# Down projections of a two-layer decoder trunk: seven products for eight, with weight sums formed by adding DMAs

## The chip, the cores and the metric

The kernel runs on one NeuronCore of a Trainium2 chip. A core has a matrix engine (TensorE, "PE" in the profile, with its weight loads listed apart as "PEld"), a vector engine (VectorE, "DVE"), a scalar engine (ScalarE, "ACT"), GpSimd ("POOL") and a sync engine ("SP") that here only issues DMAs. Each engine works through its own instructions in order and waits on semaphores for the others. Data lie in HBM, in SBUF (128 partitions) and in PSUM (128 partitions by eight banks of 512 fp32 values), where matmul results appear.

The metric is device time in microseconds, the median of several runs. The profile shows one execution.

## The reference, cut to what matters

256 tokens of width 2048 go through two layers. Layer 0 mixes by gated linear attention, layer 1 by forgetting attention; both also attend to 256 memory tokens. Behind each mixer stands the channel mixer that matters here:

```python
def conv_ffn(h, w_up, conv_w, conv_b, w_down):
    u = causal_dwconv(h @ w_up, conv_w, conv_b)
    a, val = split_cols(u, [FFN_HIDDEN, FFN_HIDDEN])     # 5632 each
    return (jax.nn.silu(a) * val) @ w_down               # (256, 5632) @ (5632, 2048)
...
for i in range(DEPTH):                                   # 2 layers
    ...
    x = x + gla_mixer(...) or fox_mixer(...)
    h = rmsnorm(x, norm_ffn[i])
    x = x + conv_ffn(h, ffn_w_up[i], ffn_conv_w[i], ffn_conv_b[i], ffn_w_down[i])
return rmsnorm(x, norm_final)
```

All inputs and the output are fp32. The weights are far larger than the activations: each is read once from HBM and used for 256 tokens.

## The kernel before

**Precision.** A matmul takes a rounded fp32 type (fp32r). To keep fp32 accuracy every operand is split into a rounded part "hi" and the rest "lo", and a product is made of three: hi·hi, hi·lo and lo·hi. Weights come from one array `wp` in HBM, laid out in the order of use, in units of 128 x 1024 values (512 KB). `load_unit` (line 185) issues the load of a unit into `raw` on SP (line 196) and the cast to `whi` on ScalarE (line 199); `split_unit` (line 202) adds `wlo = raw - whi` on VectorE (line 208). `raw` has four buffers, `whi` and `wlo` three each.

**Projections.** `proj_fm` (line 211) gives its result with features on the partitions: weights are the stationary operand, the two halves of the activations (256 tokens hi, 256 tokens lo) the moving one; lines 233, 234 and 236 are its matmuls. `proj_tm` (line 246) gives tokens on the partitions: 128 tokens of a chunk are stationary, 512 columns of a weight unit move; for each chunk of 128 inputs and each of two token halves it issues three matmuls (lines 270 to 272) into one PSUM bank per token half.

**Channel mixer.** `ffn` (line 780) takes the 44 chunks of hidden features in three parts of 16, 16 and 12 (`PARTS`). In a part it first runs one up projection per chunk (`proj_fm`, gate and value side by side), then convolution, SiLU and product (lines 795 to 805), and `split` (lines 296 and 297) writes hi and lo of the chunk into the buffer `m`. After the last chunk of the part `add_out` (line 771) runs the down projection in four column blocks of 512: `proj_tm`, and then one addition of a PSUM bank into the residual `x[f]` per token half (line 774). In the last part of a layer a callback `then` also prepares what follows: `preparing` (line 812) sums squares, transposes `x` and splits it for the next stage, and at the end of the kernel the final norm and the stores (line 860).

**Buffers.** `bufA` and `bufB` are 16 tiles each of 128 x 2 x 256, and change roles between stages: one holds the input of a projection, the other takes the next activations. `mk` and `mv` hold memory keys and values of both layers for the whole kernel. `fox` (line 674) keeps its values in `vt`, which first serves as a stash for the transposed residual.

**Order.** The program is traced into a scheduler that orders each engine's instructions by priority and by a simulated timeline, gives out buffers in that order, and inserts the semaphore waits. `tc.high_priority(offset=AHEAD)` (line 203) moves loads and splits of weights 300 places ahead, so that they run as early as buffers allow. All weight loads go through SP's queue. GpSimd only clears a few tiles.

Of the kernel before, what the change touches and what calls it, by code (L numbers as in the profile page):

```python
# [12 lines left out]
F32 = mybir.dt.float32  # L13
# [27 lines left out]
OG_EARLY = 2  # L41
WARM = 8

FV_PARTS = ((0, 376), (376, 764), (764, 1152), (1152, 1536))


# [8 lines left out]
def _panels():  # L55

    full = list(range(KC))
    out = []  # L60

    def fm(key, w, c0, kcs=full, second=None):
        cols = [(c0, 256)] if second is None else [(c0, 128), (second, 128)]
        out.append((key, w, kcs, cols, 4))

    def tm(key, w, c0, n, kcs=full, more=()):
        out.append((key, w, kcs, [(c0, n), *more], 2))

    for l in range(2):
# [36 lines left out]
    for f in range(4):  # L106
        tm(("wo", 1, f), ("fox_w_out", 0), f * 512, 512, late)
    ffn(1)
    return out

# [21 lines left out]
C_N = C_BF + 1  # L132

M_ID, M_ONE, M_FOX, M_SCAN, M_LVL = 0, 128, 256, 512, 768
M_N = M_LVL + NVER * len(LEVELS)


@with_exitstack
def _trunk(ctx: ExitStack, tc: tile.TileContext, xt, xtok, memt, wp, wgu, gns, gfin, cnv, par, msk, out):
# [9 lines left out]

    gains = const.tile([P, G_N], F32, name="gains")  # L150
    part = const.tile([P, C_N], F32, name="part")
    mask = const.tile([P, M_N], F32, name="mask")
    ident = mask[:, M_ID : M_ID + P]
    ones = mask[:, M_ONE : M_ONE + P]
    foxmask = mask[:, M_FOX : M_FOX + T]
    scanmask = mask[:, M_SCAN : M_SCAN + T]

    def gain(name, i):
        c = C_GAIN[name] + i
# [3 lines left out]
    nc.gpsimd.memset(eps, EPS)  # L163

    x = [const.tile([P, 2, 512], F32, name=f"x{f}") for f in range(4)]
    bufA = [const.tile([P, 2, T], F32R, name=f"A{i}") for i in range(KC)]
    bufB = [const.tile([P, 2, T], F32R, name=f"B{i}") for i in range(KC)]
    mk = [const.tile([P, MEM_H, T], F32, name=f"mk{l}") for l in range(2)]
    mv = [const.tile([P, 2, MEM_H * HD], F32, name=f"mv{l}") for l in range(2)]


    with tc.high_priority(offset=2 * AHEAD):
        V.memset(bufB[KC - 1].bitcast(F32), 0.0)
        warm = pwork.tile([P, 512], F32, name="ps_o", tag="o", bufs=1)
        for i in range(WARM):
            TE.matmul(warm, bufB[KC - 1][:, 0, :P], bufB[KC - 1], start=i == 0, stop=i == WARM - 1)
# [69 lines left out]
    def proj_tm(key, src, evac, spare=None):  # L246
# [9 lines left out]
        for i in range(len(units) + ahead):  # L256
            for b, u in ((0, i), (1, i - ahead)):
# [14 lines left out]
                    TE.matmul(a, xk[:, 1, xs], hi[:, s], start=False, stop=last)  # L272
                if u == len(units) - 1:
                    evac(b, a)

    def turned(pool, bank, width, col):

# [132 lines left out]

    nrm = Norm(D, "m")
    nx = StreamNorm()
    with tc.tile_pool(name="load", bufs=1) as lp:
        mraw = [lp.tile([P, KC + 4 * T], F32, name=f"mt{i}") for i in range(4)]
        mt = [t[:, KC:].rearrange("p (c t) -> p c t", t=T) for t in mraw]
# [53 lines left out]
        with tc.issue_after(loads[-1].ins):  # L469
            for i in range(KC):  # L470
                nc.sync.dma_start(xf[i], xt[i])
            nc.sync.dma_start(part, par)
            nc.sync.dma_start(mask[:, M_FOX:], msk[:, M_FOX:])
        proj_tm(("mv", 0), bufA, mv_out(0))
        for i in range(KC):
            split(bufB, i, xf[i], gain("mix0", i))
        for j in range(2):
            proj_fm(("mk", 1, j), bufA, mk_out(1, j))
            if j == 0:
# [3 lines left out]
                for f in range(4):  # L483
                    for b in range(2):
                        nx.add(f, b)
        proj_tm(("mv", 1), bufA, mv_out(1))


    def gla(nx):
        h, mix = bufB, bufA  # L490
        with tc.tile_pool(name="gla", bufs=1) as gp:
# [53 lines left out]
            def core(hd, q, k, v, bc):  # L545
# [43 lines left out]
                for li, B in enumerate(LEVELS):  # L589
# [28 lines left out]
                    m3 = mask[:, M_LVL + NVER * li : M_LVL + NVER * (li + 1)].bitcast(I32)  # L618
# [52 lines left out]
                take_og(j)  # L671


    def fox(nx, vt):
        hk, hq, mix = bufB, bufA, bufB
        stash = vt.rearrange("p b (i t) -> p (b i) t", t=T)
        with (
            tc.tile_pool(name="fox", bufs=1) as fp,
            tc.tile_pool(name="foxd", bufs=1, space=bass.MemoryType.DRAM) as dp,
        ):  # L680
            cdram = dp.tile([FOX_H, T], F32, name="cdram")
            kt = fp.tile([P, FOX_H, T], F32, name="fkt")
            for j in range(6):
                proj_fm(("fk", j), hk, lambda c, a, j=j: V.tensor_tensor(kt[:, 2 * j + c, :], whole(a), nx.row(), ALU.mult))
                for i in range(2 * j, 2 * j + 2):
                    split(hq, i, stash[:, i, :], gain("mix1", i))
# [43 lines left out]
            def attend(hd, q):  # L730
# [7 lines left out]
                TE.matmul(ps[:, :P], q[:, :P], kt[:, hd, :P], start=True, stop=True)  # L738
                TE.matmul(ps[:, P : 3 * P], q[:, P:], kt[:, hd, :], start=True, stop=True)  # L739
                pt = work("t")  # L740
                for b in range(2):
                    n = (b + 1) * P
# [25 lines left out]
                take_q(j)  # L768


    def add_out(key, src, then=None, spare=None):
        for f in range(4):
            def evac(b, a, f=f):
# [3 lines left out]

            proj_tm((*key, f), src, evac, spare if f == 3 else None)

    def ffn(l, nx, h, m, then, spare=None):  # L780
        with tc.tile_pool(name=f"ffn{l}", bufs=1) as fp:
            cw = fp.tile([P, 4 * 88], F32, name="cw")
            nc.sync.dma_start(cw, cnv[l])
            us = [fp.tile([P, T + 2], F32, name=f"u{i}") for i in range(4)]
# [3 lines left out]
            for p, (lo, hi) in enumerate(PARTS):  # L788
                for j in range(lo, hi):
                    cv = {}  # L790

                    def evac(c, a, j=j, cv=cv, i=j - lo):
# [9 lines left out]
                        cv[c] = r  # L802
                        if c == 1:
                            S.activation(cv[0], cv[0], AF.Silu)
# [4 lines left out]
                end = p == len(PARTS) - 1  # L809
                add_out(("down", l, p), m, then if end else None, spare if end else None)  # L810

    def preparing(name, dst, also=None):
        n = StreamNorm()

        def then(f, b):
            n.add(f, b)
            if b == 0:
                return
            for i in range(4 * f, 4 * f + 4, 2):
                ps = work("s", 2)  # L820
# [10 lines left out]
        return n, then  # L831

    gla(nx)
    n, then = preparing("ffn0", bufB)
    add_out(("wo", 0), bufA, then)
    with tc.tile_pool(name="stash", bufs=1) as st:
        vt = st.tile([P, 2, FOX_H * HD], F32, name="fvt")

        def also(i, ps):
            if i < 12:  # L840
                S.activation(vt.rearrange("p b t -> p (b t)")[:, i * T : (i + 2) * T], ps, AF.Copy)
            else:
                for j in range(2):
                    split(bufA, i + j, ps[:, j * T : (j + 1) * T], gain("mix1", i + j))

        n2, then = preparing("kv", bufB, also)
        ffn(0, n, bufB, bufA, then)
        fox(n2, vt)
    n, then = preparing("ffn1", bufA)
    add_out(("wo", 1), bufB, then)  # L850


    fin = StreamNorm()
    with tc.tile_pool(name="store", bufs=1) as op:
        gf = op.tile([P, D], F32, name="gf")
        nc.sync.dma_start(gf, gfin.to_broadcast([P, D]))
        y = op.tile([P, 2, 512], F32, name="y")
        junk = op.tile([P, 1], F32, name="junk")

        def then(f, b):  # L860
            fin.add(f, b)
            if f == 0 and b == 0:
                S.activation(junk, fin.sums[:, 0, 0:1], AF.Sqrt)
            dst = y if f == 3 else x[f]
            V.tensor_tensor(dst[:, b, :], x[f][:, b, :], gf[:, f * 512 : (f + 1) * 512], ALU.mult)
            if f < 3:
# [7 lines left out]
            V.reciprocal(r, r)  # L874
            fin.newton(r, v, 1)
            for g in range(4):
                t = y[:, b, :] if g == 3 else x[g][:, b, :]
# [6 lines left out]
        ffn(1, n, bufA, bufB, then, op)  # L884


def _constants():
# [66 lines left out]
```

## Time and profile before

| | |
|---|---|
| median of 3 runs | 2302.16 us (2302.14 to 2302.43) |
| span of the profiled execution (first to last instruction) | 2300.7 us; the median lies 1.5 us above it |
| granted TensorE clock | 0.999 of full speed |
| bytes read from HBM | 425.87 MB |
| weight loads of 512 KB issued by SP | 743 |
| instructions | 33144 |

The first number of a group's row is its busy time, the second the mean duration of one, and behind the bar stands the idle time of the engine just before these instructions, with what ended it ("<-"). A row of the stage table gives, for a window, the busy time of each engine and the count of instructions in parentheses, the granted clock, the mean busy share of the 16 DMA engines, and GB/s. Matmuls overlap in the engine, so that the sum of their durations is more than the time they take. Down projections run at about 658 to 745, 924 to 1012, 1146 to 1211, 1740 to 1828, 2005 to 2093 and 2226 to 2292 us.

### The profile page before, as it was taken

What the parts mean: (1) busy time and instruction counts of PE and PEld (TensorE: products, weight loads), DVE (VectorE), ACT (ScalarE), POOL (GpSimd) and SP (SyncE); (2) the same over time, 40 slices, a digit from 0 to 9 for tenths busy, and PEclk for the clock granted to TensorE, in tenths of its full rate; (3) what the DMA queues carried; (4) which work ended last, traced back from release to release, by engine and by line L of the source; (5) the groups of instructions that cost most, each with busy time, mean ns of one, the idle gap of its engine ahead of it and who ended that gap; (6) DMA issues with size and microseconds to landing.
All of it is one profiled execution on the core that took longest, in us unless ns stands there. A gap on an engine that the chain in (4) does not pass through costs nothing.

```text
span 2300.7 us, 33144 instructions
## 1 busy us (share of the span) xinstructions
PE 2286.8 (99%) x12392; PEld 1977.8 (86%) x12392; DVE 1614.6 (70%) x2639; ACT 1252.9 (54%) x1961; POOL 3.0 (0%) x19
## 2 busy tenths in 40 slices
PE   9999999999999999999999999999999999999998
PEld 7889888888888888888888998888888888888886
DVE  7568987577765777557767557657776577756775
ACT  7555565555553555445565555556554455534554
POOL 0000000000000000000000000000000000000000
PEclk9999999999999999999999999999999999999999
DMA  8644455555555555555555564555555555555554
GB/s 317 196 160 160 150 165 177 187 182 190 190 190 194 187 191 189 192 191 189 190 183 185 180 194 158 166 191 188 186 191 192 192 187 189 190 195 191 186 190 156
DMA packets 124745, 430.15 MB, mean 187 GB/s; under 512 B 14108, under 2 KB 18600, under 8 KB 124456
## 3 DMA queue, kind: packets, MB, share of 16 engines
q1 hardware_dynamic: 124152, 427.24, 55.7%
q8 instruction: 97, 1.59, 0.3%
q10 hardware_dynamic: 432, 0.79, 0.1%
q14 instruction: 64, 0.52, 0.1%
HBM read 425.87 MB, written 2.11 MB: 186 GB/s over the span
## 4 chain that ended last, share of the span: by engine, by line
PE 99%; DMA 0%; ACT 0%; DVE 0%; issue 0%; SPq 0%; DVEq 0%; ACTq 0%
PE acc L233 37%; PE acc L234 20%; PE acc L271 12%; PE acc L272 12%; PE acc L270 12%; PE acc L236 2%; PE ps_s L825 0%; PE ps_s L614 0%; PE ps_t L388 0%; PE ps_s L395 0%; PE ps_o L406 0%; DMA mt<-memt 0%; PE ps_s L739 0%; PE ps_o L633 0%; PE ps_o L755 0%; PE ps_s L533 0%
## 5 line engine op out<-in xcount | busy, mean ns | idle before, releaser
L208 DVE TENSOR_TENSOR wlo<-raw,whi 128x1024 fp32r<-128x1024 f32 (+4 forms) x812 | 972.7, 1199 | 547.3 <-ACT whi L199 533.3
L199 ACT ACTIVATE whi<-raw 128x1024 fp32r<-128x1024 f32 (+4 forms) x812 | 843.5, 1040 | 775.7 <-PE acc L272 370.6
L233 PE MATMUL acc<-B,whi 128*128 128x512 f32 x1980 | 684.1, 396 | 0.0
L233 PE MATMUL acc<-A,whi 128*128 128x512 f32 x1680 | 579.1, 396 | 1.9 <-DVE A L300 1.5
L234 PE MATMUL acc<-B,wlo 128*128 128x256 f32 x2112 | 551.2, 281 | 0.0
L234 PE MATMUL acc<-A,wlo 128*128 128x256 f32 x1792 | 463.9, 281 | 0.7 <-DVE wlo L208 0.7
L233 PEld LDWEIGHTS acc<-B,whi 128*128 128x128 f32 x1980 | 360.9, 188 | 69.0
L234 PEld LDWEIGHTS acc<-B,wlo 128*128 128x128 f32 x2112 | 397.7, 188 | 21.7
L234 PEld LDWEIGHTS acc<-A,wlo 128*128 128x128 f32 x1792 | 337.3, 188 | 21.6 <-DVE wlo L208 1.7
L233 PEld LDWEIGHTS acc<-A,whi 128*128 128x128 f32 x1680 | 304.9, 188 | 58.8 <-DVE A L300 1.9
L271 PE MATMUL acc<-wlo,B 128*128 128x512 f32 (+3 forms) x736 | 274.9, 374 | 1.2 <-DVE wlo L208 1.2
L272 PE MATMUL acc<-whi,B 128*128 128x512 f32 (+3 forms) x736 | 274.0, 373 | 0.0
L270 PE MATMUL acc<-whi,B 128*128 128x512 f32 (+3 forms) x736 | 247.6, 372 | 0.0
L271 PE MATMUL acc<-wlo,A 128*128 128x512 f32 x544 | 212.6, 391 | 0.0
L272 PE MATMUL acc<-whi,A 128*128 128x512 f32 x544 | 211.8, 389 | 0.0
L270 PE MATMUL acc<-whi,A 128*128 128x512 f32 x544 | 192.6, 391 | 0.0
L241 ACT ACTIVATE part<-acc 128x256 f32<-128x256 f32 x240 | 90.0, 375 | 163.1 <-PE acc L236 163.1
L271 PEld LDWEIGHTS acc<-wlo,B 128*128 128x128 f32 x736 | 138.2, 188 | 21.0 <-DVE wlo L208 1.6
L272 PEld LDWEIGHTS acc<-whi,B 128*128 128x128 f32 x736 | 138.3, 188 | 18.7
L270 PEld LDWEIGHTS acc<-whi,B 128*128 128x128 f32 x736 | 137.5, 188 | 18.7
L243 DVE TENSOR_TENSOR wholes<-acc,part 128x256 f32<-128x256 f32 x240 | 101.1, 421 | 66.3 <-ACT part L241 65.9
L272 PEld LDWEIGHTS acc<-whi,A 128*128 128x128 f32 x544 | 102.2, 188 | 21.2
(201 smaller groups left out, 1571.2 us busy)
## 6 DMA issues: line engine op xcount, KB each, us to landing
raw<-wp SPq DMA_DIRECT2D x743, 512.0 KB, 3.5
raw<-wp SPq DMA_DIRECT2D x32, 384.0 KB, 3.1
raw<-wp SPq DMA_DIRECT2D x24, 388.0 KB, 3.5
raw<-wp SPq DMA_DIRECT2D x8, 400.0 KB, 3.0
xf<-xt SPq DMA_DIRECT2D x16, 128.0 KB, 4.5
x<-xtok SPq DMA_DIRECT2D x4, 512.0 KB, 6.7
mt<-memt SPq DMA_DIRECT2D x3, 512.0 KB, 7.1
cb<-cdram SPq DMA_DIRECT2D x12, 128.0 KB, 3.3
```

Source lines behind the costliest of these rows:

```text
L199: casts.append(S.activation(hi[:, s], raw[:, s], AF.Copy))
L208: V.tensor_tensor(lo[:, s], raw[:, s], hi[:, s].bitcast(F32), ALU.subtract)
L233: TE.matmul(a, hi[:, s], both, start=done == 0, stop=False)
L234: TE.matmul(a[:, :T], lo[:, s], both[:, 0, :], start=False, stop=False)
L236: TE.matmul(a, hi[:, s], both, start=False, stop=True)
L241: S.activation(t, a[:, T:], AF.Copy)
L243: V.tensor_tensor(r, a[:, :T], t, ALU.add)
L270: TE.matmul(a, xk[:, 0, xs], hi[:, s], start=u == 0 and j == 0, stop=False)
L271: TE.matmul(a, xk[:, 0, xs], lo[:, s], start=False, stop=False)
L272: TE.matmul(a, xk[:, 1, xs], hi[:, s], start=False, stop=last)
```

## The change

The down projection is done as a 2 x 2 block product with seven products in place of eight. The blocks are: two token halves of 128; chunks taken in pairs (a first and a second one); and columns in two halves of 512 out of 1024. For one pair the activations are F0, F1 (first chunk, token halves 0 and 1) and S0, S1 (second chunk), the weights W00, W01 (first chunk, column halves 0 and 1) and W10, W11. The products are numbered:

| product | activations | weights | added to (column half, token half) |
|---|---|---|---|
| 1 | F0 - F1 + S1 | W11 + W10 + W00 | +(0,0) +(1,1) |
| 2 | S1 | W00 + W10 | +(0,1) -(1,1) |
| 3 | F0 | W01 | +(1,0) +(1,1) |
| 4 | F1 - S1 | W00 | +(0,0) +(0,1) |
| 5 | S0 | W11 | -(0,0) +(1,0) |
| 6 | F1 - F0 | W11 + W10 + W00 + W01 | +(1,1) |
| 7 | S0 - F0 + F1 - S1 | W11 + W10 | +(0,0) |

Products are summed over all pairs of a part in PSUM, each in a bank of its own (four from `pacc`, and the banks "o", "t" and "s"), and then added into or subtracted from `x`.

The activation sums are made once per pair in the up stage (`Pairs`): seven blocks of 128 x 128, split together. The weight sums are made for two pairs at a time (a group: four chunks, blocks of 128 x 2 x 512): `CHAINS` lists three buffers. Into "far" the block of product 5 is loaded by SP, cast and split; then GpSimd issues a DMA that adds the next block to the same buffer (`accum_op=ALU.add`), the sum is cast and split for product 7, and so on for 1 and 6. "near" makes 4 and then 2; "raw" makes 3. Each cast uses the same `whi` and `wlo` buffers as before, three of each.

To make room, `bufA` and `bufB` become slices of one tile `arena`; a pool `late` with two buffers ("annex") holds what no longer fits; the mask used by linear attention and the memory keys and values move to a pool closed after that mixer, those of layer 1 being spilled to HBM by GpSimd and loaded again by SP at the start of `fox`. The down projection of the last part no longer runs its first token half four units ahead (`spare`).

```diff
+PAIR = 7 * P
+CHAINS = (("far", 3, ((5, 1, 1), (7, 1, 0), (1, 0, 0), (6, 0, 1))),
+          ("raw", 4, ((3, 0, 1),)),
+          ("near", 2, ((4, 0, 0), (2, 1, 0))))
+QUAD_BUFS = {"acc": 4, "s": 2}
+QUAD_ORDER = (5, 3, 4, 2, 7, 1, 6)
+QUAD_SLOT = {1: 5, 2: 2, 3: 0, 4: 4, 5: 1, 6: 3, 7: 6}
+QUAD_OUT = {1: ((0, 0, 1), (1, 1, 1)), 2: ((0, 1, 1), (1, 1, -1)), 3: ((1, 0, 1), (1, 1, 1)),
+            4: ((0, 0, 1), (0, 1, 1)), 5: ((0, 0, -1), (1, 0, 1)), 6: ((1, 1, 1),), 7: ((0, 0, 1),)}
...
-            for f in range(4):
-                tm(("down", l, p, f), ("ffn_w_down", l), f * 512, 512, list(range(lo, hi)))
+            for f in range(2):
+                quad(("down", l, p, f), ("ffn_w_down", l), f * 1024, list(range(lo // 2, hi // 2)))
...
-    bufA = [const.tile([P, 2, T], F32R, name=f"A{i}") for i in range(KC)]
-    bufB = [const.tile([P, 2, T], F32R, name=f"B{i}") for i in range(KC)]
-    mk = [const.tile([P, MEM_H, T], F32, name=f"mk{l}") for l in range(2)]
-    mv = [const.tile([P, 2, MEM_H * HD], F32, name=f"mv{l}") for l in range(2)]
+    arena = const.tile([P, ARENA], F32R, name="arena")
...
+    def halves(raw):
+        hi = wpool.tile([P, NUNIT], F32R, name="whi", tag="whi", bufs=3)
+        S.activation(hi, raw, AF.Copy)
+        lo = wpool.tile([P, NUNIT], F32R, name="wlo", tag="wlo", bufs=3)
+        V.tensor_tensor(lo, raw, hi.bitcast(F32), ALU.subtract)
+        return hi, lo
+
+    def proj_quad(pool, key, src, evac):
...
+        for g in range(groups):
+            parts = {}
+            with tc.high_priority(offset=AHEAD):
+                for tag, bufs, steps in CHAINS:
+                    raw = (wpool if tag == "raw" else pool).tile([P, NUNIT], F32, name="raw", tag=tag, bufs=bufs)
+                    for i, (m, r, c) in enumerate(steps):
+                        if i:
+                            nc.gpsimd.dma_start(raw, block(g, r, c), accum_op=ALU.add)
+                        else:
+                            loads.append(nc.sync.dma_start(raw, block(g, r, c)))
+                        parts[m] = halves(raw)
+            for m in QUAD_ORDER:
+                hi, lo = parts[m]
+                for j in range(2):
+                    s = slice(j * 512, (j + 1) * 512)
+                    both = src[2 * g + j]
+                    xh, xl = (h[:, QUAD_SLOT[m], :] for h in both)
+                    last = g == groups - 1 and j == 1
+                    TE.matmul(acc[m], xh, hi[:, s], start=g == 0 and j == 0, stop=False)
+                    TE.matmul(acc[m], xh, lo[:, s], start=False, stop=False)
+                    TE.matmul(acc[m], xl, hi[:, s], start=False, stop=last)
+                if g == groups - 1:
+                    evac(m, acc[m])
...
+    class Pairs:
...
+            V.tensor_tensor(q[:, 3:5, :], q[:, 7:8, :].to_broadcast([P, 2, P]), q[:, 0:3:2, :], ALU.subtract)
+            V.tensor_tensor(q[:, 5, :], q[:, 0, :], q[:, 4, :], ALU.subtract)
+            V.tensor_tensor(q[:, 6, :], q[:, 1, :], q[:, 5, :], ALU.subtract)
+            hi, lo = self.dst[p]
+            S.activation(hi, q[:, :7, :], AF.Copy)
+            V.tensor_tensor(lo, q[:, :7, :], hi.bitcast(F32), ALU.subtract)
...
+        nc.gpsimd.dma_start(spill[0], mk[1].rearrange("p h t -> p (h t)"))
+        nc.gpsimd.dma_start(spill[1], mv[1].rearrange("p b c -> p (b c)"))
...
+            nc.sync.dma_start(mk[1].rearrange("p h t -> p (h t)"), spill[0])
+            nc.sync.dma_start(mv[1].rearrange("p b c -> p (b c)"), spill[1])
...
+    def add_quads(pool, key, src, then=None):
+        for f in range(2):
+            def evac(m, a, f=f):
+                for c, b, sign in QUAD_OUT[m]:
+                    o = x[2 * f + c][:, b, :]
+                    V.tensor_tensor(o, o, a, ALU.add if sign > 0 else ALU.subtract)
...
+            proj_quad(pool, (*key, f), src, evac)
...
-                            V.tensor_tensor(r, cv[0], r, ALU.mult)
-                            split(m, i, r)
+                            g, r = (t.rearrange("p (b t) -> p b t", b=2) for t in (cv[0], r))
+                            V.tensor_tensor(m.place(i), g, r, ALU.mult)
+                            m.placed(i)
...
-                add_out(("down", l, p), m, then if end else None, spare if end else None)
+                add_quads(fp, ("down", l, p), dst, then if p == len(PARTS) - 1 else None)
```

More of the change, by code (lines that the diff above doesn't have):

```diff
@@ L67, in tm, with quad @@
         out.append((key, w, kcs, [(c0, n), *more], 2))
+    def quad(key, w, c0, pairs):
+        for g in range(0, len(pairs), 2):
+            for r in range(2):
+                for c in range(2):
+                    rows = [2 * p + r for p in pairs[g : g + 2]]
+                    out.append(((*key, g // 2, r, c), w, rows, [(c0 + c * 512, 512)], 2))
     for l in range(2):
@@ L274, in proj_tm, with block @@
                     evac(b, a)
+    def halves(raw):
[5 more added lines that the diff above has]
+    def proj_quad(pool, key, src, evac):
+        groups = len([k for k in where if k[: len(key)] == key]) // 4
+        acc = {}
+        for m, tag in zip((5, 3, 4, 2, 7, 1, 6), ("acc", "acc", "acc", "acc", "o", "t", "s")):
+            bank = pacc if tag == "acc" else pwork
+            acc[m] = bank.tile([P, 512], F32, name="quad", tag=tag, bufs=QUAD_BUFS.get(tag, 1))
+        def block(g, r, c):
+            off, _, _ = where[(*key, g, r, c)][0]
+            return wp[off : off + P * NUNIT].rearrange("(p n) -> p n", p=P)
+        for g in range(groups):
[21 more added lines that the diff above has]
+                    evac(m, acc[m])
@@ L833, in _trunk, with annex, twos, also @@
     gla(nx)
+    memory.close()
     n, then = preparing("ffn0", bufB)
     add_out(("wo", 0), bufA, then)
-    with tc.tile_pool(name="stash", bufs=1) as st:
-        vt = st.tile([P, 2, FOX_H * HD], F32, name="fvt")
-        def also(i, ps):
+    late = ctx.enter_context(tc.tile_pool(name="late", bufs=1))
+    def annex(i, dtype=F32R):
+        return late.tile([P, ANNEX[i]], dtype, name="annex", tag=f"annex{i}")
+    def twos(t):
+        return list(zip(t[::2], t[1::2]))
+    mix0 = twos(pairs(arena, KC * 512, 9) + pairs(annex(0), 0, 3) + pairs(annex(1), 0, 4))
+    mix1 = twos(pairs(arena, 0, 16))
+    stash = []
+    def also(i, ps):
+        if not stash:
+            t = annex(1, F32)
+            stash.extend(t[:, j * T : (j + 1) * T] for j in range(12))
+        for j in range(2):
             if i < 12:
-                S.activation(vt.rearrange("p b t -> p (b t)")[:, i * T : (i + 2) * T], ps, AF.Copy)
+                S.activation(stash[i + j], ps[:, j * T : (j + 1) * T], AF.Copy)
             else:
[L843 to L849, printed above, removed]
+                split(bufA, i + j, ps[:, j * T : (j + 1) * T], gain("mix1", i + j))
+    n2, then = preparing("kv", bufB, also)
+    ffn(0, n, bufB, mix0, then)
+    fox(n2, stash, bufA)
+    h1 = chunks(arena, 28, 4) + chunks(annex(0), 0, 5) + chunks(annex(1), 0, 7)
+    n, then = preparing("ffn1", h1)
     add_out(("wo", 1), bufB, then)
@@ L876, in then @@
             for g in range(4):
-                t = y[:, b, :] if g == 3 else x[g][:, b, :]
+                t = (y[0] if g == 3 else x[g])[:, b, :]
                 if g == 1:
```

89 lines of the change are left out of this document (66 added, 23 removed).

## The prediction

> **What bounds the kernel now.** I read the first page from the top (busy shares, chain), then the stage table, then the down projections alone. The page's busy line, its chain and its DMA queue line:
>
> ```profile
> PE 2286.8 (99%) x12392; PEld 1977.8 (86%) x12392; DVE 1614.6 (70%) x2639; ACT 1252.9 (54%) x1961; POOL 3.0 (0%) x19
> ...
> q1 hardware_dynamic: 124152, 427.24, 55.7%
> ...
> PE 99%; DMA 0%; ACT 0%; DVE 0%; issue 0%; SPq 0%; DVEq 0%; ACTq 0%
> ```
>
> TensorE is the bound everywhere: 99% of the span, 99% of the chain. POOL has 19 instructions; GpSimd issues no DMA at all, so no accumulating transfer appears in this trace. By stage (columns: window, length, busy time of PE, PEld, DVE, ACT, POOL, granted clock, DMA share, GB/s), two down stages and an up stage:
>
> ```profile
> 660.00:744.00 84.00, 84.00 (x372) 69.57 (x371) 44.57 (x45) 34.56 (x36) 0.00 (x0) 1.00 0.58 192
> ...
> 1742.00:1826.00 84.00, 84.00 (x373) 69.55 (x372) 44.37 (x45) 34.11 (x34) 0.00 (x0) 1.00 0.58 193
> 540.00:640.00 100.00, 100.00 (x575) 87.30 (x574) 79.01 (x126) 58.49 (x90) 0.00 (x0) 1.00 0.57 188
> ```
>
> In a down stage VectorE is busy 53%, ScalarE 41%, the DMA engines 58%: all have room. How regular it is shows in the timeline of one down stage, two ScalarE casts of neighbouring weight units:
>
> ```profile
> 2029.88 1.06 ACT L199 ACTIVATE whi<-raw 128x1024 fp32r<-128x1024 f32 x1 [1.66 <-PE acc L272]
> ...
> 2032.60 1.06 ACT L199 ACTIVATE whi<-raw 128x1024 fp32r<-128x1024 f32 x1 [1.66 <-PE acc L272]
> ```
>
> One unit (two chunks by 512 columns: 2 chunks, 2 token halves, 3 matmuls, so 12) takes 2.72 us, 0.2267 us a matmul; the 389 ns that the groups show is latency, overlapped. The cast waits for PE to give back one of the three whi buffers, so casts are early and PE sets the pace.
>
> **The change, term by term.** Matmuls: now 2 layers x 44 chunks x 4 column blocks x 2 halves x 3 = 2112, which is 2112 x 0.2267 = 478.8 us. Seven products for eight leave 1848, or 418.9 us: a gain of 59.9 us if nothing else moves. A new group (four chunks by 1024 columns) is 42 matmuls, 9.52 us, where the same work takes 48 x 0.2267 = 10.88 us now. There are 2 layers x 2 x (4 + 4 + 3) = 44 groups. So every resource has 9.52 us a group to keep the gain, and 10.88 us to lose nothing.
>
> VectorE and ScalarE, from the groups by line, and from adjoining instructions in VectorE's timeline:
>
> ```profile
> L208 DVE TENSOR_TENSOR wlo<-raw,whi 128x1024 fp32r<-128x1024 f32 (+4 forms) x812 | 972.7, 1199 | 547.3 <-ACT whi L199 533.3 <-PE acc L234 1.1 <-issue 0.3
> L199 ACT ACTIVATE whi<-raw 128x1024 fp32r<-128x1024 f32 (+4 forms) x812 | 843.5, 1040 | 775.7 <-PE acc L272 370.6 <-PE acc L233 213.1 <-ACT cv L804 79.4
> L774 DVE TENSOR_TENSOR x<-x,acc 128x512 f32<-128x512 f32 x64 | 41.2, 681 | 4.8 <-PE acc L272 4.8
> ```
> ```profile
> 37.52 1.22 DVE L208 TENSOR_TENSOR wlo<-raw,whi 128x1024 fp32r<-128x1024 f32 x1
> 38.65 0.15 DVE L326 TENSOR_SCALAR nv<-ps_t 128x2 f32<-128x2 f32 x1
> ...
> 745.34 1.28 DVE L774 TENSOR_TENSOR x<-x,acc 128x512 f32<-128x512 f32 x2
> ```
>
> Back to back, a weight split holds VectorE 38.65 - 37.52 = 1.13 us and an add into x 1.28 / 2 = 0.64 us. Split units rise from 176 to 308 and adds into x from 48 to 144 (12 for each 1024 columns of a part, 4 before). Per part and half of the columns VectorE then needs 28 x 1.13 + 12 x 0.64 = 39.3 us against 38.1 us of PE (four groups), 31.4 against 28.6 (three): 2 x 2 x (39.3 + 39.3 + 31.4) = 440 us in all. VectorE therefore ties with PE in the down stages, and alone would leave 478.8 - 440 = 38.7 us of gain, more where the last adds of a part run under the next up stage. ScalarE needs 7 x 1.06 = 7.4 us of 9.52: hidden. In the up stages each pair of chunks gets three small VectorE operations and one wider split, about 1.3 us more by the rows above scaled to width, in two up blocks of 11.1 us (575 matmuls at 64 a block in the 100 us row above); VectorE is at 79% there, so I cost it at nothing (uncovered: 44 x 1.3 = 57 us).
>
> DMA decides. The fastest stretch of this trace, and the landing times of the weight loads (the line of the tile raw):
>
> ```profile
> 8.00:16.00 8.00, 7.58 (x42) 5.99 (x41) 7.94 (x18) 8.00 (x19) 0.00 (x0) 1.00 1.03 418
> ```
> ```profile
> raw<-wp SPq DMA_DIRECT2D x743, 512.0 KB, 3.5
> ```
> ```profile
> DMA to landing us min/median/max: 2.7/3.5/8.3
> ```
>
> At 418 GB/s a 512 KB block (524288 bytes) occupies the 16 engines 1.25 us. A group now loads four blocks; afterwards three plain and four adding ones. An adding DMA has to read the block that lies in SBUF as well as the one in HBM. No row shows one, so: lower bound 1.25 us (the second read is free), upper bound 3.5 us (the whole median landing of a plain block, with nothing overlapped), and I take 2.5 us, twice the bytes read at the rate shown, because the sum cannot be formed without that second read. A group is then 3 x 1.25 + 4 x 2.5 = 13.75 us of DMA, 605 us for 44. What is loaded ahead during the up stages comes off: buffers for nine first blocks (far 3, raw 4, near 2), 9 x 1.25 x 6 stages = 67.5 us. 605 - 67.5 - 478.8 = +58.7 us against now.
>
> The Trainium skill, "Collectives: The Full Stack", in "The bandwidth ceiling: the fold count and why AG ≠ RS ≠ AR", says that a transfer which adds issues two reads per chunk on the same ring and so runs at about half the rate of a copy; by it the adding block is 2.5 us and the sum the one above. The same skill, "DMA: Bandwidth & Descriptors", in "Anatomy of one DMA — SWDGE (gpsimd) path", fits a GpSimd DMA with 2.0 us plus bytes at 436 GB/s, 3.2 us for this block, with nothing extra for an add; by that alone the group is 8.75 us of DMA and the first rival holds. No run here shows either yet.
>
> Order. The four blocks of the far chain go into one buffer one after another: load, cast, add, cast, add, cast, add, cast. Each add waits on POOL for both halves of the cast before; behind it in POOL's queue stand the other chain's adds, and behind the next cast on ScalarE and VectorE all later casts. One link is 3.5 us to land (bounds 2.7 and 8.3) + 1.06 + 1.23 = 5.8 us, while a product is 1.36 us. Products 7, 1 and 6 are such links and stand next to each other in the written order. What can cover them is other groups' products. That the planner does move other work between such steps is seen in PE's timeline, where attention's matmuls stand inside a projection:
>
> ```profile
> 1367.01 0.28 PE L234 MATMUL acc<-A,wlo 128*128 128x256 f32 x1
> 1367.13 1.02 PE L395 MATMUL ps_s<-mk,mq 128*128 128x256 f32 x4
> 1367.80 0.58 PE L233 MATMUL acc<-A,whi 128*128 128x512 f32 x1
> ```
>
> With three far buffers, so three chains in flight, I cost the links at nothing inside a stage; at the very end of the kernel no other work follows, and two links stay bare: 2 x (5.8 - 1.36) = +8.9 us.
>
> The rest is small and I cost it at nothing: SP issues 132 loads in place of 176; two spills on POOL in the first projection and two reloads on SP before the fox stage are 512 KB each, with the engines 57% busy; POOL's memsets precede them or come long after. The arena replaces 32 tiles; if tracking went by whole tile, each of the 44 pair splits would stop PE for 1.06 + 1.23 us, 101 us; the slices are disjoint, so nothing.
>
> Sum: 2300.7 + 58.7 + 8.9 = 2368.3 us of span, and the median of the runs is 1.5 us above the span now (2302.16): 2370 us.
>
> **The rivals.**
> 1. Faster: adds ride as cheap as plain loads and the order covers the chains. DMA is 8.75 us a group, under PE's 9.52; VectorE and PE set the pace. Between -38.7 + 8.9 and -59.9 + 8.9: 2251 to 2272 us, say 2260. For it: 42% of the DMA time is free. It decides from an adding block's cost below (10.88 + 67.5 / 44 - 3.75) / 4 = 2.2 us, if the links stay hidden. Against it: it needs PE, VectorE and DMA, each at 80 to 100% of a stage, to stay in step with three buffers.
> 2. The chains are bare: casts keep the written order, so ScalarE and VectorE wait for an add with later casts queued behind it. One bare link a group: (9.52 + 4.44) x 44 - 478.8 = +136 us, 2438 us; both: +331 us, 2633 us. It decides above 10.88 - 9.52 = 1.36 us of bare wait a group. For it: three whi and wlo buffers, one POOL queue. Against it: the interleaving above.
> 3. An adding block costs the full 3.5 us: 17.75 x 44 - 67.5 - 478.8 = +235 us, 2537 us plus the end.
> 4. Gain and stalls cancel: 2298 to 2307 us.
>
> **How the numbers follow.** The forecast (2320 to 2420) gets 0.42, rival 1 0.30, rival 2 0.13, rival 3 0.11, rival 4 0.04. Faster by over 0.2% is rival 1, 0.30; same 0.04; slower 0.66. 0.2% is 4.6 us, about what runs of this kernel (0.3 us apart here) on different chips can tell. The range is 2252 to 2560: below it lies the fastest part of rival 1 (0.05), above it both links bare or dearer adds still (0.12). The likeliest case's own range is 2320 to 2420.
>
> **What would show it.** Right: DMA share in the down stages 0.9 or more with a group near 13 us, matmul gaps there ended by casts that wait for DMA into raw, PE below 97% of the span; 1848 matmuls of the down projections at the old pitch; up stages unchanged at 11.1 us a block. Wrong: DMA share of 0.7 with VectorE near 100% in the down stages (rival 1); DMA share low, and casts waiting for DMA one after the other while POOL waits for VectorE (rival 2); up stages longer (VectorE's cover gone).

## The result, and the profile after

The changed kernel takes 3439.6 us (median of four runs, 3432.1 to 3444.0) where the kernel before took 2302.15 us on the same chip: a ratio of 1.494, 95% interval 1.4915 to 1.4958. The forecast was 2370 us, the range ended at 2560: the sign was right, the size was wrong by 1070 us.

The profiled execution has a span of 3433.7 us. From the page of the changed kernel: busy times, the granted clock in 40 slices, the two DMA queues, the groups of the new projection's casts and splits, and the landing times of the two kinds of load:

```profile
PE 2622.5 (76%) x12128; PEld 2103.9 (61%) x12128; DVE 1868.1 (54%) x2955; ACT 1385.9 (40%) x2056; POOL 155.9 (5%) x197
...
PEclk9999999966699666897679999996669976679766
...
q1 hardware_dynamic: 118248, 405.22, 34.9%
q0 software_dynamic: 25632, 93.33, 16.1%
...
L307 DVE TENSOR_TENSOR wlo<-raw,whi 128x1024 fp32r<-128x1024 f32 x308 | 366.5, 1222 | 1044.0 <-ACT whi L305 1044.0
...
L305 ACT ACTIVATE whi<-raw 128x1024 fp32r<-128x1024 f32 x308 | 311.6, 1050 | 1207.2 <-DMA raw<-wp 1201.6
...
raw<-wp SPq DMA_DIRECT2D x699, 512.0 KB, 3.5
raw<-wp POOLq DMA_DIRECT2D x176, 512.0 KB, 5.3
```

TensorE has 264 matmuls fewer (12392 to 12128), as the seven products promise, but it is busy for 76% of the span instead of 99%, and in six stretches the granted clock falls to 0.6. Those are the six down stages. From the first to the last matmul of each, they took 479.9 us together before and take 1603.7 us now, or 36.4 us for each of the 44 groups, where the prediction has 10.88 us before. The rest of the span went from 1820.8 to 1830.0 us. So +1123.8 of the +1133 us of span lie in the down projections.

What waits there is the next view, the waits of the changed kernel (engine, what it was about to do, what released it: us in total, times, longest):

```profile
POOL raw L329 <- DVE wlo L307: 2554.1, 174, 258.4
ACT whi L305 <- DMA raw<-wp: 1201.6, 176, 9.9
DVE wlo L307 <- ACT whi L305: 1044.0, 182, 9.3
...
PE quad L340 <- ACT whi L305: 739.3, 237, 6.4
```

It is a circle. ScalarE waits 176 times for a transfer into raw, 6.8 us each (1201.6 / 176), and there are just 176 adding transfers: by the trace every one of them is waited for. VectorE waits for ScalarE, GpSimd's next add waits for VectorE, TensorE waits for the cast. (GpSimd's total also holds the up stages, in which it has nothing to do.) TensorE's lower clock is not in this circle: of the 1207.2 us that ScalarE idles before these casts 1201.6 end with a transfer, and all 1044.0 us before the splits end with a cast, so hardly any cast or split waits for TensorE to give a buffer back.

The timelines of one group show one turn of this circle after another. GpSimd, which issues the adds (start, duration, in brackets the idle time before and its releaser):

```profile
803.20 0.86 POOL L329 DMA_DIRECT2D raw<-wp  x1 [11.08 <-DVE wlo L307]
811.30 0.86 POOL L329 DMA_DIRECT2D raw<-wp  x1 [7.24 <-DVE wlo L307]
819.18 0.87 POOL L329 DMA_DIRECT2D raw<-wp  x1 [7.03 <-DVE wlo L307]
829.40 0.86 POOL L329 DMA_DIRECT2D raw<-wp  x1 [9.35 <-DVE wlo L307]
840.27 0.86 POOL L329 DMA_DIRECT2D raw<-wp  x1 [10.01 <-DVE wlo L307]
```

ScalarE, which casts:

```profile
808.69 1.06 ACT L305 ACTIVATE whi<-raw 128x1024 fp32r<-128x1024 f32 x1 [7.83 <-DMA raw<-wp]
816.58 1.06 ACT L305 ACTIVATE whi<-raw 128x1024 fp32r<-128x1024 f32 x1 [6.83 <-DMA raw<-wp]
824.52 2.95 ACT L305 ACTIVATE whi<-raw 128x1024 fp32r<-128x1024 f32 x3 [6.89 <-DMA raw<-wp]
836.52 2.00 ACT L305 ACTIVATE whi<-raw 128x1024 fp32r<-128x1024 f32 x2 [9.05 <-DMA raw<-wp]
```

VectorE, which splits:

```profile
809.77 1.23 DVE L307 TENSOR_TENSOR wlo<-raw,whi 128x1024 fp32r<-128x1024 f32 x1 [3.18 <-ACT whi L305]
817.66 1.23 DVE L307 TENSOR_TENSOR wlo<-raw,whi 128x1024 fp32r<-128x1024 f32 x1 [6.66 <-ACT whi L305]
```

Read one link across the three: the add is issued at 803.20, the cast of its result starts at 808.69 (5.5 us), the split runs from 809.77 to 811.00, the next add is issued at 811.30. A link costs 8.1 us and the next 7.9, 10.2 and 10.9: together 37.07 us, one group. The counts at the end of ScalarE's lines give the order: one cast (7), one (1), three (6, then 3 and 4), two (2, and 5 of the next group). That is the order in which CHAINS is written, 5, 7, 1, 6, 3, 4, 2, and here two adds are never under way at once. Nothing of the next group but its first cast comes ahead.

The windows of the changed kernel, with the columns of the prediction's stage table: that group, two short pieces of it, and an up stage for comparison:

```profile
803.20:840.27 37.07, 18.51 (x42) 11.72 (x41) 11.26 (x12) 7.07 (x7) 3.44 (x5) 0.64 0.45 94
```
```profile
813.50:817.50 4.00, 0.06 (x1) 0.00 (x0) 0.00 (x0) 0.92 (x1) 0.00 (x0) 0.50 0.53 103
817.70:821.00 3.30, 2.83 (x6) 1.76 (x6) 1.19 (x1) 0.00 (x0) 0.87 (x1) 0.50 0.13 12
```
```profile
1010.00:1100.00 90.00, 90.00 (x518) 78.62 (x517) 75.19 (x122) 53.03 (x77) 0.00 (x0) 1.00 0.57 189
```

The group does its 42 matmuls in 37.07 us; no engine is busy for more than half of it, and the DMA engines have a share of 0.45. That is how a chain of dependences looks: nothing is full. The up stage is as before, TensorE at 100% and 0.57 of the DMA engines.

### The profile page after: what moved, and what is told of

Read it like the earlier page. It is cut to its first block, busy times and chain, and to the rows that moved or that the text cites. A ratio compares the mean times of both kernels' runs of the same rounds, so it can differ in the third digit from the quotient of the medians.

```text
span 3433.7 us, 33498 instructions
## 1 busy us (share of the span) xinstructions
PE 2622.5 (76%) x12128; PEld 2103.9 (61%) x12128; DVE 1868.1 (54%) x2955; ACT 1385.9 (40%) x2056; POOL 155.9 (5%) x197
## 3 DMA queue, kind: packets, MB, share of 16 engines
q1 hardware_dynamic: 118248, 405.22, 34.9%
q0 software_dynamic: 25632, 93.33, 16.1%
## 5 line engine op out<-in xcount | busy, mean ns | idle before, releaser
L260 PE MATMUL acc<-arena,whi 128*128 128x512 f32 x2692 | 939.0, 397 | 3.8 <-ACT whi L226 2.1
L307 DVE TENSOR_TENSOR wlo<-raw,whi 128x1024 fp32r<-128x1024 f32 x308 | 366.5, 1222 | 1044.0 <-ACT whi L305 1044.0
L340 PE MATMUL quad<-whi,arena 128*128 128x512 f32 x518 | 334.5, 646 | 674.7 <-ACT whi L305 672.0
L305 ACT ACTIVATE whi<-raw 128x1024 fp32r<-128x1024 f32 x308 | 311.6, 1050 | 1207.2 <-DMA raw<-wp 1201.6
L261 PE MATMUL acc<-arena,wlo 128*128 128x256 f32 x2848 | 753.3, 282 | 1.2 <-DVE wlo L235 1.2
L261 PEld LDWEIGHTS acc<-arena,wlo 128*128 128x128 f32 x2848 | 537.9, 189 | 30.4 <-DVE wlo L235 2.5
L260 PEld LDWEIGHTS acc<-arena,whi 128*128 128x128 f32 x2692 | 494.4, 188 | 100.4 <-ACT whi L226 4.8
L341 PE MATMUL quad<-wlo,arena 128*128 128x512 f32 x518 | 303.2, 585 | 40.4 <-DVE wlo L307 40.4
L260 PE MATMUL acc<-annex,whi 128*128 128x512 f32 x968 | 331.4, 395 | 0.0
L342 PE MATMUL quad<-whi,arena 128*128 128x512 f32 x476 | 260.9, 548 | 0.0
L299 PE MATMUL acc<-whi,arena 128*128 128x512 f32 (+3 forms) x576 | 211.7, 368 | 0.0
L297 PE MATMUL acc<-whi,arena 128*128 128x512 f32 (+3 forms) x576 | 192.8, 368 | 0.0
L260 PEld LDWEIGHTS acc<-annex,whi 128*128 128x128 f32 x968 | 172.5, 188 | 31.8
```

The costliest lines, as they stand in the source:

```text
L260: TE.matmul(a, hi[:, s], both, start=done == 0, stop=False)
L261: TE.matmul(a[:, :T], lo[:, s], both[:, 0, :], start=False, stop=False)
L297: TE.matmul(a, xk[:, 0, xs], hi[:, s], start=u == 0 and j == 0, stop=False)
L305: S.activation(hi, raw, AF.Copy)
L307: V.tensor_tensor(lo, raw, hi.bitcast(F32), ALU.subtract)
L340: TE.matmul(acc[m], xh, hi[:, s], start=g == 0 and j == 0, stop=False)
```

## The experiments

Two theories stood after this. **Links**: each adding transfer is a serial step of about 8 us because casts keep the written order, and the time is four steps a group. **Adding transfers**: they are dear in themselves. The first four runs take away the add, the links, or the order. Runs 1, 3, 6 and 8 are single executions; the other times are medians of four.

**1. The links stay, the add goes.** POOL's transfers overwrite instead of adding:

```diff
-                            nc.gpsimd.dma_start(raw, block(g, r, c), accum_op=ALU.add)
+                            nc.gpsimd.dma_start(raw, block(g, r, c))
```

> The four adding DMAs of a group become plain ones from the same queue into the same buffer; the waits between load, cast and next load stay, the sums are left out. If the time goes into bare links (each DMA waits for the cast before it, and the next cast for that DMA, with nothing else to do), only the landing gets shorter, from 5.3 us to some 3.5 to 4: 176 x 1.3 to 1.8 us = 230 to 320 us less, 3120 to 3210 us. If the adds' load on the DMA engines is the cause, the kernel falls to 2300 us or below. If the seven products themselves (banks, added splits, arena) are the cause, it stays at 3440 us.

Measured: 3154.7 us; the down stages take 1324.7 us, 30.1 us a group. From its page, queue and landing time:

```profile
q0 software_dynamic: 25632, 93.33, 9.0%
...
raw<-wp POOLq DMA_DIRECT2D x176, 512.0 KB, 3.8
```

A plain transfer in the same place lands in 3.8 us instead of 5.3, and the time falls by 285 us, 1.62 us for each of 176 links, about the difference in landing. 853 of the 1137 us are still there, with no adding transfer in the kernel. The add is the smaller part.

**2. The links go.** Each product loads its own block through SP:

```diff
-                for tag, bufs, steps in CHAINS:
...
+                for m in QUAD_ORDER:
+                    raw = wpool.tile([P, NUNIT], F32, name="raw", tag="raw", bufs=4)
+                    loads.append(nc.sync.dma_start(raw, block(g, *where_is[m])))
+                    parts[m] = halves(raw)
```

> Each of the seven products loads one block by a plain DMA of SP into a buffer of its own, casts in the order of the products; the sums are left out, everything else of the change stays. Bare links as the cause: PE and VectorE set the pace, 2302 less 30 to 51 us, 2251 to 2272 us. DMA load by the adds as the cause: the same. Seven products themselves as the cause: above 3300 us.

Measured: 2400.5 us, ratio 1.042 (1.0407 to 1.0438); 13.0 us a group. A down stage of it, in the windows:

```profile
670.00:750.00 80.00, 67.15 (x261) 46.44 (x259) 60.68 (x60) 47.48 (x45) 0.00 (x0) 1.00 0.86 283
```

Of the 1137 us, 1039 are gone with the links and the clock is back at 1.00. But the expected gain did not come: TensorE is busy 67 of 80 us, and ScalarE still waits for transfers into raw, 155.3 us over the run. Either four buffers are too few or something else is full; that is run 7.

**3. Only the written order changes.** Casts are written in the order of the products, and the adds stay:

```diff
-                for tag, bufs, steps in CHAINS:
-                    raw = ...
-                    for i, (m, r, c) in enumerate(steps):
...
+                for m in QUAD_ORDER:
+                    ...
+                    parts[m] = halves(raws[k])
+                    if i + 1 < len(steps):
+                        nc.gpsimd.dma_start(raws[k], block(g, *steps[i + 1][1:]), accum_op=ALU.add)
```

> As the changed kernel, but the casts are written in the order in which the products are used (5, 3, 4, 2, 7, 1, 6) instead of chain by chain (5, 7, 1, 6, 3, 4, 2). Bare links as the cause, and casts taking place in written order: the link 5 to 7 is then covered by 3, 4 and 2, while 4 to 2, 7 to 1 and 1 to 6 stay bare, three in place of four of about 8 us: some 300 us less, about 3150 us. If the planner reorders casts freely, or the DMA load is the cause: unchanged, 3440 us.

Measured: 3225.2 us, 31.8 us a group. With 3 and 4 between the first two steps of the far chain one link is covered, and 4.6 us a group go. The buffers, the transfers and the matmuls are the same, so the written order sets part of the time. It was expected 75 us faster, with three bare links a group. Three there are: casts wait for an adding transfer 132 times (three in each of the 44 groups; in the change 176 times), for 6.9 us each (904.4 us in all).

**4. Two groups are interleaved.** Casts and products of neighbouring groups are written in turn, so that four other products stand between two steps of a far chain; buffers and transfers as in the change:

```diff
+STEP = {5: 0, 7: 5, 1: 10, 6: 15, 3: 2, 4: 6, 2: 11}
...
-        for g in range(groups):
...
+        for n, m in sorted(((n, m) for n in range(2 * groups) for m in STEP), key=lambda x: 7 * x[0] + STEP[x[1]]):
...
+                hi, lo = halves(raw)
+                if i + 1 < len(steps):
+                    nc.gpsimd.dma_start(raw, block(n, *steps[i + 1][1:]), accum_op=ALU.add)
```

> The casts and products of neighbouring groups are written interleaved, so that four other products stand between two links of a chain; the same DMAs, casts and products. Bare links as the cause: the down stages fall to what the DMA engines or the rest of a link need, 13.75 us a group or less, 2330 to 2450 us. DMA load or POOL's queue as the cause: little changed, above 3200 us.

Measured: 2560.1 us, ratio 1.112 (1.1105 to 1.1143); 16.7 us a group. A down stage of it, then its page's lines:

```profile
690.00:770.00 80.00, 58.39 (x215) 42.46 (x215) 51.52 (x52) 35.96 (x35) 17.23 (x20) 0.94 1.02 245
```
```profile
q0 software_dynamic: 25632, 93.33, 20.1%
...
raw<-wp POOLq DMA_DIRECT2D x176, 512.0 KB, 7.3
```

Written in another order, the same work loses 880 us: this is the strongest evidence that the order is the cause. And the stage now has another bound: the DMA engines have a share of 1.02, while they move only 245 GB/s. (The share is the time that packets took over the time of 16 engines, so that it can read a little over 1.) The expectation was missed. An adding block holds the engines longer than I had taken: 20.1% of 2556.2 us for 176 blocks is 2.92 us each (the two spilled blocks, about 1% of the queue, are counted in); and run 6 shows that this is not all of it.

**5. Interleaved, with plain transfers.**

```diff
-                    nc.gpsimd.dma_start(raw, block(n, *steps[i + 1][1:]), accum_op=ALU.add)
+                    nc.gpsimd.dma_start(raw, block(n, *steps[i + 1][1:]))
```

> The interleaved order of e4 with plain DMAs in place of the adding ones (sums left out), same queue, buffers and waits. In e4 the DMA engines are at 0.99 to 1.02 of their time in the down stages. If the second read of an add sets e4's time, a group of 16.6 us falls to the 12 to 13 us of seven plain loads: 44 x 4 = 160 to 190 us less, 2370 to 2400 us. If what is left of the links sets it, only the landing time goes: some 2500 us.

Measured: 2395.5 us, ratio 1.041 (1.0394 to 1.0425); 13.1 us a group.

```profile
690.00:750.00 60.00, 51.98 (x203) 37.58 (x201) 48.37 (x50) 33.45 (x33) 10.26 (x19) 0.97 0.91 305
```

The number of packets and bytes is the same as in run 4, the share falls below 1 (0.91), and 3.6 us a group go, as the case of the second read had it. So the adds cost run 4 3.6 us a group: they hold the engines longer (the queue's share is 20.1% of the span there, 11.7% here) and land later (7.3 us for 4.9), and the run does not part the two.

**6. Interleaved, with one buffer more for the far chain** and wider steps (adds kept):

```diff
-STEP = {5: 0, 7: 5, 1: 10, 6: 15, 3: 2, 4: 6, 2: 11}
-CHAINS = (("far", 3, ...), ("raw", 4, ...), ...)
+STEP = {5: 0, 7: 6, 1: 12, 6: 18, 3: 3, 4: 1, 2: 9}
+CHAINS = (("far", 4, ...), ("raw", 3, ...), ...)
```

> As e4 with adds, but four far buffers in place of three and five other products between two links in place of four; raw has three buffers in place of four to make room, everywhere. If the engines' time sets e4: unchanged within 1%, 2540 to 2590 us. If links are still bare in e4: 2450 us or less.

Measured: 2500.7 us, 15.2 us a group, between the two cases that were named.

```profile
690.00:770.00 80.00, 63.07 (x227) 44.53 (x225) 56.85 (x59) 38.82 (x38) 18.14 (x21) 0.91 1.03 264
```

The engines stay full and move 264 GB/s instead of 245. So a full share did not set run 4 alone; some of its time was still order or buffers. Buffers and steps were changed together, so which of them gave the 59 us is open. This is the fastest version that computes the whole result, and it is still 8.6% behind the kernel before (2500.7 / 2302.15, a single execution).

**7. No links, and nine block buffers**, as many as the change has. Every other block of run 2 goes into five buffers of its own:

```diff
-                    raw = wpool.tile([P, NUNIT], F32, name="raw", tag="raw", bufs=4)
+                    own = n % 2 == 0
+                    raw = (pool if own else wpool).tile([P, NUNIT], F32, name="raw", tag="far" if own else "raw",
+                                                        bufs=5 if own else 4)
```

> As e2 (every product loads its own block by a plain DMA, sums left out), with nine buffers for blocks in place of four. e2 stands 98 us above the kernel before with casts waiting for loads. If that is too few buffers for a load's round trip: the down stages fall to the pace of PE and VectorE, 2251 to 2275 us, under the kernel before. If DMA rate (0.87 busy in e2) or VectorE sets e2: 2370 us or more.

Measured: 2319.2 us, ratio 1.0072 (1.0055 to 1.0089): still no gain, and between the two cases that were named. Of run 2's 98 us 81 go with the buffers, so four were too few. The down stages take 484.8 us, 11.0 us a group. A stage of it in the windows, then VectorE's groups by line between 665 and 730 us, and a piece of its timeline:

```profile
940.00:1010.00 70.00, 66.12 (x274) 49.52 (x272) 65.05 (x67) 48.40 (x46) 0.00 (x0) 1.00 0.94 343
```
```profile
L307 DVE TENSOR_TENSOR wlo<-raw,whi 128x1024 fp32r<-128x1024 f32 x44 | 52.5, 1222 | 4.5 <-ACT whi L305 3.9
...
L888 DVE TENSOR_TENSOR x<-x,quad 128x512 f32<-128x512 f32 x12 | 7.7, 681 | 0.0
```
```profile
689.90 1.22 DVE L307 TENSOR_TENSOR wlo<-raw,whi 128x1024 fp32r<-128x1024 f32 x1
691.04 1.28 DVE L888 TENSOR_TENSOR x<-x,quad 128x512 f32<-128x512 f32 x2
692.23 1.22 DVE L307 TENSOR_TENSOR wlo<-raw,whi 128x1024 fp32r<-128x1024 f32 x1
```

VectorE is busy 65.05 of 70 us. Seven splits of 1.19 us (52.5 / 44) and 3.3 adds of 0.64 us (144 adds in 44 groups) are 10.4 us of busy time a group. Back to back the timeline has a split in 1.14 us (691.04 - 689.90) and an add in 0.60 (half of 692.23 - 691.04), which is 9.9 us a group. Either way it is more than the 9.52 us of matmuls: VectorE now has more to do than TensorE, with the DMA engines at 0.94 close behind. So in this order and with these buffers the change would not have won even with free sums of blocks.

**8. Two links instead of four.** Products 1 and 6 get a plain block of their own:

```diff
-CHAINS = (("far", 3, ((5, 1, 1), (7, 1, 0), (1, 0, 0), (6, 0, 1))),
+CHAINS = (("far", 3, ((5, 1, 1), (7, 1, 0))), ("raw", 4, ((1, 0, 0),)), ("raw", 4, ((6, 0, 1),)),
```

> The changed kernel with the far chain cut: 5 and then 7 by an add, but the blocks of 1 and 6 loaded plain into buffers of their own (their sums left out); near stays. Two adds a group in place of four, order of casts as in the changed kernel. Bare links at 8 to 12 us each as the cause: half of the 36.4 us of a group goes, about 44 x 17 = 750 us less, 2640 to 2750 us. Load of the adds on the engines as the cause: 5 plain and 2 adding in place of 3 and 4, about a fifth of the down stages, 3100 us.

Measured: 2926.2 us, 24.9 us a group. A down stage of it:

```profile
700.00:800.00 100.00, 57.95 (x168) 41.44 (x168) 41.04 (x40) 28.29 (x28) 6.88 (x8) 0.73 0.58 147
```

The links are half as many and cost the same each: casts wait 88 times for an adding transfer, 6.7 us each (586.1 us), where it was 176 times 6.8. The expectation took the whole 36.4 us of a group for links and halved it, but a group without links still takes 13.0 us (run 2) or 11.0 (run 7). With none (run 2), two and four links it is 13.0, 24.9 and 36.4 us, nearly a straight line of 5.9 us a link; counted from run 7, which has as many buffers as this run, the first two cost 7.0 each. The two links that are left belong to different chains and still do not run beside each other: GpSimd issues its adds 9.1 us or more apart, and they land after 5.7 us (median).

**9. Fewer adds into x.** Run 7 with one add into x for each of the products 1 to 5, which leaves out 5 of the 12 adds (the output lacks these terms as well as the sums of blocks):

```diff
+QUAD_OUT = {m: v[:1] for m, v in QUAD_OUT.items()}
```

> As e7 (no links, plain loads, nine block buffers), with one addition into x for each product in place of two for products 1 to 5: 7 of 12 per half of the columns and part stay, so the output lacks those terms. In e7 VectorE is 93% busy in the down stages and they take 86 us, as before the change. If VectorE's added work sets e7, 5 x 0.64 us go from each of 12 halves, 38 us: 2275 to 2290 us, the first of these kernels under the one before. If the DMA engines (0.95 busy in e7) set it: unchanged, 2315 to 2322 us.

Measured: 2288.0 us, ratio 0.9936 (0.9919 to 0.9952); the down stages take 459.6 us.

```profile
665.00:730.00 65.00, 64.27 (x271) 48.85 (x270) 59.94 (x59) 48.19 (x47) 0.00 (x0) 1.00 0.97 357
```

With 5 x 12 = 60 adds of 0.64 us out of the way (38 us in all, if every one counted) 31 us go, as the case of VectorE had it, and the time is for the first time below the kernel before, by 0.6%. So VectorE's work held run 7 back by that much. The DMA engines did not hold run 7 at 0.94, since they move more here. TensorE is nearly full here (64.27 of 65 us) and so are the DMA engines (0.97, 357 GB/s); 14 us is what is then left of the 59.9.

**The account.** Of the 1137 us, 17 are there with no links and no adds (run 7), 836 come with links of plain transfers (run 1 less run 7, which also casts in the order of the products and loads through SP alone), and 285 with the add (the change less run 1).

## Why the prediction was wrong

- **Order: the step that failed.** "I cost the links at nothing inside a stage" rested on attention's matmuls that stand inside a projection in the trace before, and on three far buffers, "so three chains in flight". The interleaving seen there was of different stages; between casts of the same loop the changed kernel's trace shows the written order, and there three buffers let no two chains run side by side, since the cast of the next chain's first block stands behind the last cast of this group. Runs 3 and 4 change only the order and win 214 and 880 us. In place of nothing the term is 19.7 us a group: 36.4 in the change less 16.7 in run 4, which differs from it in the order alone.
- **Rival 2 named the mechanism** and its sign in the profile, low DMA share, "casts waiting for DMA one after the other while POOL waits for VectorE": share 0.45, 176 such waits. It was mis-sized. It counted one or two bare links a group; there are four, since 7, 1 and 6 follow each other in one buffer and 2 waits behind 4. And it priced a link at 5.8 us less 1.36; issue to issue it is 7.9 to 10.9 us, other work included, and 5.9 us by the line through runs 2, 8 and the change (6.4 counted from run 7). Four times 4.44 would have given 27.3 us a group; measured are 36.4. The chance of 0.13 was too small by the same misreading.
- **DMA: right in kind, too low, and not what acted.** The forecast's own sign, a share of 0.9 or more near 13 us a group, did not appear in the changed kernel. It appears in runs 4 and 6, at 16.7 and 15.2 us a group for the predicted 13.75. The factor of two is right: by the queue's share an adding block holds the engines 3.14 us (16.1% of 3433.7 us over 176), a plain one from the same queue 1.61 us (run 1: 9.0% of 3152.9), a ratio of 1.95. The base was low: 1.25 us came from the one fastest stretch of the trace before. The Trainium skill, "Collectives: The Full Stack", section "The bandwidth ceiling: the fold count and why AG ≠ RS ≠ AR", has the reduce step of a ring run at half the rate of a copy, because the add needs two source reads; the ratio of 1.95 here agrees. The 67.5 us of loading ahead are not gained: three plain blocks of 1.55 us (34.9% of 3433.7 us over 773 blocks' worth of bytes) and four of 2.92 are 16.3 us a group in run 4, with 16.7 measured, because the engines are not full at the ends of a stage (in the first one the share is 0.82 from 658 to 680 us and 0.64 from 780 to 792).
- **VectorE: the work was right, the tie was not free.** 440 us alone was predicted, 10.0 us a group. Run 7's timeline has 9.9 back to back, so the prices hold, yet its down stages take 484.8 us, 11.0 a group: VectorE is idle for 7% of the time, and ScalarE's casts wait 106.7 us for TensorE to give a whi buffer back. The prediction had named this against rival 1 (three engines "to stay in step with three buffers") but put no price on it. In run 7's order the 2251 to 2272 us of rival 1, which had 0.30, are not reached even without links and adds; whether another order reaches them is open.
- **What held.** The 264 matmuls fewer; ScalarE hidden; the up stages: what is outside the down stages grew by 9.2 us, of which 7.1 lie after the last matmul (9.1 to 16.2 us), where the prediction had put 8.9 for bare links. The links are not the cause: run 7 has none, and 15.4 us after its last matmul. What is, stays open. The slices of the arena cost nothing (TensorE at 100% in the up stage), nor do the spills. The matmuls kept their old pitch only where the links are away (0.229 us from start to start in run 7, 0.427 in the changed kernel, medians).
- **The sign** was right for the wrong reason: the adds as load were to make the kernel slower, but in the changed kernel the engines' share is 0.45 and load is not the limit. What the adds cost there, 285 us, they cost by landing later within a link.

## What to carry to other kernels

A transfer that adds into a buffer which was just cast is a round trip through four engines (transfer, cast, split, issue), and it is hidden only if other work stands between two of them in the written order of every engine on the way. That more buffers alone do not help while the casts are queued in chain order follows from that order; no run gave the far chain more buffers and nothing else. So search the trace before for two casts of the same loop that have changed places; if none have, price every link bare. And when an algorithm saves work on the engine that is full, work out the next two: here seven products for eight took 12.5% of the stage's matmuls and left VectorE with about 10 us of work for 9.52 us of matmuls and the DMA engines at a share of 0.94.

## What the runs showed that was not expected

- **A chain that stops TensorE also slows it.** The granted clock reads 0.50 in the pieces 813.50 to 817.50 and 817.70 to 821.00 us above, with a pause and a burst of six matmuls in turn. TensorE's timeline of the changed kernel:

```profile
811.65 0.63 PE L342 MATMUL quad<-whi,arena 128*128 128x512 f32 x1
812.08 0.63 PE L340 MATMUL quad<-whi,arena 128*128 128x512 f32 x1
812.50 0.63 PE L341 MATMUL quad<-wlo,arena 128*128 128x512 f32 x1
812.93 0.63 PE L342 MATMUL quad<-whi,arena 128*128 128x512 f32 x1
817.68 0.79 PE L340 MATMUL quad<-whi,arena 128*128 128x512 f32 x1 [4.13 <-ACT whi L305]
```

  One matmul follows another after 0.43 us, not 0.2267 us. So the busy time of TensorE rose from 2286.8 to 2622.5 us with fewer matmuls, and a busy share of 76% overstates its work. The Trainium skill, "TensorE: Matmul & The Clock Gate", section "🔬 Part 1: The HAM clock gate (the "warmup" mystery)", has the clock at half after at least one idle window of about 3.4 us; the granted clock of 0.50 in the pause of 4.13 us and in the burst behind it, at 817.68 us, agrees.
- **The price of an add in the queue.** A 512 KB transfer that adds landed in 5.3 us, a plain one in its place in 3.8 us; with the engines full, in run 4, the add took 7.3 us. In the windows shown, engines at a share of 1.02 and 1.03 moved 245 and 264 GB/s with four adds in seven blocks (runs 4 and 6), and at 0.94 and 0.97 they moved 343 and 357 GB/s with plain blocks alone (runs 7 and 9).
